# Strassen's seven block products in place of eight in a hybrid decoder step on one Trainium2 core

## The chip, the cores and the metric

The kernel runs on one core of a Trainium2 chip. A core has a matrix engine (TensorE, PE in the profile, with its weight loads as PEld), a vector engine (VectorE, DVE), a scalar engine (ScalarE, ACT), a general engine (GpSimd, POOL) and a queue that starts transfers (SyncE, SP). Each engine takes its own instructions in the order in which they were written, and waits on semaphores for the others. The metric is the device time of one execution in microseconds (us); less is better. Before the change it is 1356.34 us, the median of 3 runs from 1355.4 to 1358.23.

## The reference

One layer of a hybrid decoder, for 1024 prompt tokens and 32 sample tokens (8 sequences of 4), all in float32:

```python
def hybrid_layer(x, conv_state, ssm_state, mem_k, mem_v, ...):
    hn = rmsnorm(x, norm_g)
    proj = jnp.einsum('btd,de->bte', hn, w_in)      # 1024 -> 7696 columns
    gm_uv, gm_gate, ssm_z, ssm_xbc, ssm_dt, mem_q, mem_gate = jnp.split(proj, SPLIT_POINTS, axis=-1)
    a_out, v_rows = gmlp_branch(gm_uv, ...)          # gelu, layernorm of v, mix in 128-token chunks, u * mixed
    a_out = a_out * jax.nn.silu(gm_gate)
    b_out, ssm_new, conv_new = mamba2_branch(ssm_z, ssm_xbc, ssm_dt, conv_state, ssm_state, ...)
    c_out = memory_branch(mem_q, mem_gate, mem_k, mem_v)
    mixed = jnp.concatenate([a_out, b_out, c_out], axis=-1)
    y = x + jnp.einsum('bte,ed->btd', mixed, w_out)  # 3072 -> 1024 columns
```

`mamba2_branch` runs a causal convolution of width 4 over the 1536 columns of xbc, then an exact scan over 8 chunks of 128 tokens for 16 heads. `memory_branch` attends to 256 memory tokens, whose keys and values are projected here too. A final RMSNorm follows.

## The kernel before

**Products.** Every float32 operand of a large product is split by `split` (L104) into a float32r part H and a remainder L: ScalarE copies H, VectorE or GpSimd subtracts it. `gemm3` (L286) then does H*H, L*H and H*L for every 128 rows of the contraction, so three matmuls for each of its 8 steps of k. `gemmA` keeps the weights of one channel tile (128 channels) stationary and streams the 1056 tokens in three blocks of 352; `gemmB` keeps 128 tokens stationary and streams 256 channels. Weights arrive as 0.5 MB units (`w_load`), in the order of the list `wseq`, and are split one or two units ahead of their use (`w_tick`, `w_half`). The normed input xH, xL stays in SBUF.

**Stages.** In order: norm of the input with the z and dt columns (`z_unit`); the 12 channel tiles of xbc with the convolution (`conv_evac`, `conv_finish`); the 23 channel tiles of q, of the gate gg and of seven eighths of the gate mg, which `spill` sends to DRAM; v (`gemmB`, results stay in SBUF as vt); u with the mix of the gMLP (`mix`); the last tile of mg; the output projection of branch A (`outproj` with first=True), which puts y in DRAM; keys and values of the memory; the output projection of B, which adds to y; that of C with the residual and the final norm.

**Work beside the products.** `hook` is called after every step of k of a large product. It adds `pace["rate"]` to a counter, and for every whole one it steps a generator in `side`. Under q, gg and mg run, at 0.43 steps a hook, the chunked scan (`scan`: 16 chunk-and-group parts of 7 steps), the scan of the sample tokens (`sample_scan`) and the attention of the sample tokens against their caches (`sample_att`). The order of all instructions is that in which this Python code writes them (`manual_schedule`). So an instruction that waits on an engine holds all that stands behind it there.

**Banks.** `mm()` rotates over three PSUM banks for the large products; `sd()` over four for the side work.

**The lines that the steps touch.** In a channel tile of xbc, ScalarE takes each block out of PSUM twice (L646, L650), VectorE adds three shifted products of 1024 tokens (L659), and ScalarE applies Silu over the result (L664), which waits for them. In a part of the scan, GpSimd does the scale of the gated norm (L240, L241), the remainder of the scaled inputs (L110 xdL), the skip term (L775), the decay of the state (L877) and the scaled inputs of the next part (L782, whose buffer VectorE's L888 releases).

## Time and profile before

| what | value |
| --- | --- |
| time, median of 3 runs | 1356.34 us |
| span of the profiled execution | 1351.7 us |
| time around the span (median less span) | 4.6 us |
| TensorE busy | 1320.8 us, 98% |
| VectorE busy | 590.4 us, 44% |
| ScalarE busy | 496.5 us, 37% |
| GpSimd busy | 210.4 us, 16% |
| moved by DMA | 151.44 MB, 112 GB/s on average |

The profiled execution's own time is taken as its span of 1351.7 us and 4.6 us around it. Busy time of TensorE is counted from the start of a matmul to its modelled end; matmuls are pipelined, so the distance between the starts of two of them is shorter than the duration of one. The granted clock of TensorE reads 9 tenths or more in all 40 slices of the span.

### The profile page before, as it was taken

The numbers are of one execution on the slowest core, as the hardware profiler recorded it, in microseconds if no ns is written. First come the engines' busy times: TensorE is split into PE (matmuls) and PEld (weight loads), VectorE is DVE, ScalarE is ACT, GpSimd is POOL, SyncE is SP. The second block draws the span as 40 slices with busy tenths as digits, with TensorE's granted clock in tenths as the row PEclk, the third lists the DMA queues.
The fourth block names the chain that finished last, engine by engine and source line by source line (L and its number), as shares of the span: only waits on it lengthen the run. The fifth ranks groups of instructions, "written<-read, shape, count | busy, mean of one in ns | idle before, by whom it ended". The sixth has DMA issues, their size and how long they took to land. (4 is left out here: it accounts for less than half of the span.)

```text
span 1351.7 us, 22582 instructions
## 1 busy us (share of the span) xinstructions
PE 1320.8 (98%) x9231; PEld 1236.4 (91%) x9231; DVE 590.4 (44%) x943; ACT 496.5 (37%) x962; POOL 210.4 (16%) x274
## 2 busy tenths in 40 slices
PE   8999999999999999999999999999999889999996
PEld 7999999988888898888779999998999889999996
DVE  6212545566767632422112245345312646654543
ACT  6323444464545432222211124344313633322322
POOL 4200000043434424200000010002000600000122
PEclk9999999999999999999999999999999999999999
DMA  6223111122222245475551114221423565436432
GB/s 223 78 77 99 44 48 48 47 88 76 78 72 88 82 118 165 149 226 179 181 181 45 32 32 127 68 68 44 144 93 128 177 178 182 151 117 193 139 121 95
DMA packets 171595, 151.44 MB, mean 112 GB/s; under 512 B 13781, under 2 KB 155049, under 8 KB 171493
## 3 DMA queue, kind: packets, MB, share of 16 engines
q1 hardware_dynamic: 171492, 150.01, 36.1%
q8 instruction: 72, 1.18, 0.4%
q14 instruction: 31, 0.25, 0.1%
HBM read 111.97 MB, written 37.79 MB: 111 GB/s over the span
## 5 line engine op out<-in xcount | busy, mean ns | idle before, releaser
L290 PE MATMUL ps_mm<-xH,wh 128*128 128x352 f32 x1056 | 359.9, 341 | 0.0
L292 PE MATMUL ps_mm<-xH,wl 128*128 128x352 f32 x1056 | 339.6, 322 | 0.0
L291 PE MATMUL ps_mm<-xL,wh 128*128 128x352 f32 x1056 | 339.2, 321 | 0.0
L290 PEld LDWEIGHTS ps_mm<-xH,wh 128*128 128x128 f32 x1056 | 198.3, 188 | 25.3 <-issue 21.0
L291 PEld LDWEIGHTS ps_mm<-xL,wh 128*128 128x128 f32 x1056 | 199.0, 188 | 0.7
L292 PEld LDWEIGHTS ps_mm<-xH,wl 128*128 128x128 f32 x1056 | 198.4, 188 | 0.0
L110 DVE TENSOR_TENSOR wl<-wr,wh 128x1024 fp32r<-128x1024 f32 (+2 forms) x106 | 121.8, 1161 | 175.2 <-ACT wh L107 174.8
L290 PE MATMUL ps_mm<-wh,xH 128*128 128x256 f32 (+1 forms) x512 | 148.0, 289 | 0.0
L291 PE MATMUL ps_mm<-wl,xH 128*128 128x256 f32 (+1 forms) x512 | 146.4, 286 | 0.1
L292 PE MATMUL ps_mm<-wh,xL 128*128 128x256 f32 (+1 forms) x512 | 145.6, 284 | 0.3 <-DVE xL L110 0.3
L107 ACT ACTIVATE wh<-wr 128x1024 fp32r<-128x1024 f32 (+3 forms) x113 | 101.7, 915 | 36.2 <-PE ps_mm L291 14.2
L292 PEld LDWEIGHTS ps_mm<-wh,xL 128*128 128x128 f32 x512 | 98.1, 192 | 0.6 <-DVE xL L110 0.5
L290 PEld LDWEIGHTS ps_mm<-wh,xH 128*128 128x128 f32 x512 | 97.8, 191 | 0.4
L291 PEld LDWEIGHTS ps_mm<-wl,xH 128*128 128x128 f32 x512 | 97.7, 191 | 0.4 <-POOL wl L110 0.4
L701 ACT ACTIVATE gt<-ps_mm 128x352 f32<-128x352 f32 x72 | 33.0, 458 | 98.2 <-PE ps_mm L292 77.1
L290 PE MATMUL ps_mm<-aH,wh 128*128 128x384 f32 (+1 forms) x192 | 62.7, 327 | 1.9 <-ACT gt L1403 1.0
L290 PE MATMUL ps_mm<-bH,wh 128*128 128x384 f32 (+1 forms) x192 | 64.0, 334 | 0.0
L291 PE MATMUL ps_mm<-aL,wh 128*128 128x384 f32 (+1 forms) x192 | 63.0, 328 | 0.3
L292 PE MATMUL ps_mm<-bH,wl 128*128 128x384 f32 (+1 forms) x192 | 62.4, 325 | 0.2 <-DVE wl L110 0.2
L291 PE MATMUL ps_mm<-bL,wh 128*128 128x384 f32 (+1 forms) x192 | 62.5, 326 | 0.0
L292 PE MATMUL ps_mm<-aH,wl 128*128 128x384 f32 (+1 forms) x192 | 61.9, 323 | 0.0
L1720 POOL TENSOR_TENSOR xres<-xres,gfin 128x1536 f32<-128x1536 f32 (+3 forms) x6 | 14.4, 2392 | 231.6 <-ACT junk L1714 231.6
(385 smaller groups left out, 2472.8 us busy)
## 6 DMA issues: line engine op xcount, KB each, us to landing
wr<-in_w_in_dram SPq DMA_DIRECT2D x60, 512.0 KB
wr<-in_w_out_dram SPq DMA_DIRECT2D x24, 512.0 KB
kv<-in_cache_mem_k_dram SPq DMA_DIRECT2D x16, 512.0 KB
kv<-in_cache_mem_v_dram SPq DMA_DIRECT2D x16, 512.0 KB
y_d<-gt SPq DMA_DIRECT2D x32, 192.0 KB
q_d<-gt SPq DMA_DIRECT2D x24, 176.0 KB
gg_d<-gt SPq DMA_DIRECT2D x24, 176.0 KB
mg_d<-gt SPq DMA_DIRECT2D x24, 176.0 KB
```

The costliest lines, as they stand in the source:

```text
L107: ACT.activation(out=H, in_=raw, func=AF.Copy)
L110: leng.tensor_tensor(out=L, in0=raw, in1=rb(H), op=ALU.subtract)
L290: PE.matmul(out=ps, lhsT=lH, rhs=rH, start=(first and k == k0), stop=False)
L291: PE.matmul(out=ps, lhsT=lH, rhs=rL, start=False, stop=False)
L292: PE.matmul(out=ps, lhsT=lL, rhs=rH, start=False, stop=(last and k == k0 + kn - 1))
L701: ACT.activation(out=t[:, :BLK], in_=ps[:, :BLK], func=func)
L1720: eng.tensor_tensor(out=t[:, 0:nf, c0:c0 + w], in0=t[:, 0:nf, c0:c0 + w], in1=gc.unsqueeze(1).to_broadcast([128, nf, w]), op=ALU.mult)
```

## The change

Two channel tiles of weights (256 columns) now make a unit. Its 1024 x 256 weight block and the 1024 x 1024 input are cut into 2 x 2 blocks, and Winograd's form of Strassen's algorithm makes the four output blocks (128 channels x 512 tokens) from seven products of 512 rows of contraction instead of eight. There are 26 units: 6 for xbc, 4 each for q, gg, mg and u, and 4 for the output projection of branch A. `unit` does one. GpSimd makes the four sums of weight blocks (`u_prep`); ScalarE makes the H of all seven weight operands, and L comes from VectorE for operands 0, 3 and 6 and from GpSimd for 1, 2, 4 and 5 (`u_split`); VectorE joins the products with seven additions (`add`). The input's four sums T1 to T4 are made once, beside v (`x_sums`). The 32 sample tokens no longer ride in the products: each unit multiplies them in float32, in eight matmuls that use four column groups of the array (`samp_in`), and adds the four groups up a unit later (`samp_out`).

z and v come first now, and v's rows go to DRAM (`v_d`). The convolved xs, B and C go to DRAM (`xc_d`, `bc_d`) and come back part by part of the scan (`xk_load`); the gated rows of A, B and C go through `a_d`, `yb_d` and `c_d`. In the scan, the second half of the masks moves from VectorE to GpSimd (`sM`), the minimum and the transposed output of B from VectorE to ScalarE (`sE`, `y_T2`), and the rows of decays come by transfers that GpSimd starts (`r_rows`). The side work now runs at 0.8 to 1.0 steps a hook, over ten units.

```diff
+    XBC = [(0, 1), (2, 3), (8, 10), (4, 5), (6, 7), (9, 11)]
...
+    BANK = (0, 1, 2, 0, 2, 0, 1)
...
+    def u_prep(u, step):
+        if u >= len(useq):
+            return
+        if step == 0:
+            U.t[u] = [stp.tile([128, 4, 128], F32, tag=f"st{j}", name="wst", bufs=1) for j in range(2)]
+            t1, t2 = U.t[u]
+            POOL.tensor_tensor(out=t1, in0=A_(u, 2, 1), in1=A_(u, 2, 2), op=ALU.add)
+            POOL.tensor_tensor(out=t2, in0=t1, in1=A_(u, 1, 1), op=ALU.subtract)
+        else:
+            t1, t2 = U.t[u]
+            POOL.tensor_tensor(out=t1, in0=A_(u, 1, 1), in1=A_(u, 2, 1), op=ALU.subtract)
+            POOL.tensor_tensor(out=t2, in0=A_(u, 1, 2), in1=t2, op=ALU.subtract)
...
+    def u_split(u, j):
+        if u >= len(useq):
+            return
+        src = (lambda: A_(u, 1, 1), lambda: U.t[u][0], lambda: U.t[u][1], lambda: A_(u, 1, 2),
+               lambda: U.t[u][0], lambda: U.t[u][1], lambda: A_(u, 2, 2))[j]()
+        h, l = (stp.tile([128, 4, 128], F32R, tag=f"u{e}", name=f"u{e}", bufs=SR) for e in "hl")
+        split(src, h, l, ACT, POOL if j in (1, 2, 4, 5) else DVE)
+        U.hl[u, j] = (h, l)
...
+            for j in range(4):
+                PE.matmul(out=ps[32 * j:32 * j + 32, 0:256], lhsT=xs[:, 4 * r + j, :], rhs=R[r][:, j, :],
+                          start=(r == 0), stop=(r == 1), tile_position=(0, 32 * j))
+        se = gtp.tile([128, 256], F32, tag="se", name="se", bufs=1)
...
+        def add(out, ps, nm):
+            DVE.tensor_tensor(out=out, in0=ps, in1=keep[nm], op=ALU.add)
...
+        def add_fin(i, h, ps, nm):
+            t = dst(i, h)
+            add(t, ps, nm)
+            fin(i, h, t)
+        for j in range(7):
+            ps = banks[j] = mm_bank((BANK[j] + 2 * u) % 3)
+            wH, wL = U.hl.pop((u, j))
+            H, L = X[XN[j]]
+            gemm3(ps, lambda k: (wH[:, k, :], wL[:, k, :]), lambda k: (H[:, k, :], L[:, k, :]), 0, 4, True, True)
+            if j == 0:
+                ACT.activation(out=keep["m1"], in_=ps, func=AF.Copy)
+                u_prep(u, 1)
+                u_split(u, 3)
+            elif j == 1:
+                u_split(u, 4)
+                samp_out()
+                samp_in(u, xs, done)
+                u_free()
+            elif j == 2:
+                add(keep["u"], ps, "m1")
+                add(keep["x"], banks[1], "u")
+                u_split(u, 5)
+            elif j == 3:
+                add_fin(0, 0, ps, "m1")
+                u_split(u, 6)
+                u_prep(nx, 0)
+                u_free()
+            elif j == 4:
+                add(keep["u"], ps, "u")
+                add_fin(1, 1, banks[1], "u")
+                u_split(nx, 0)
+            elif j == 5:
+                add_fin(0, 1, ps, "x")
+                u_split(nx, 1)
+            else:
+                add_fin(1, 0, ps, "u")
+                u_split(nx, 2)
+            if mids is not None and j in mids:
+                mids[j]()
...
+            for nm, tg in (("B11", "m1"), ("B12", "u"), ("B22", "x"), ("B21", "st0")):
+                t = raw[nm] = (stp.tile([128, 512], F32, tag=tg, name=tg, bufs=1).rearrange("p (k t) -> p k t", k=4)
+                               if tg != "st0" else stp.tile([128, 4, 128], F32, tag="st0", name="wst", bufs=1))
+                H, L = XO[nm]
+                POOL.tensor_tensor(out=t, in0=rb(H[:, :, cs]), in1=rb(L[:, :, cs]), op=ALU.add)
+                yield
+            b11, b12, b21, b22 = (raw[nm] for nm in ("B11", "B12", "B21", "B22"))
+            for nm, out, a, b in (("T1", b11, b12, b11), ("T3", b12, b22, b12), ("T2", b22, b22, b11),
+                                  ("T4", b21, b21, b22)):
+                POOL.tensor_tensor(out=out, in0=a, in1=b, op=ALU.subtract)
+                yield
...
+    def conv_finish(ct):
+        raw = raws.pop(ct)
         o = VO["conv_b"] + ct
...
+        d = cvp.tile([128, NP], F32, tag="cd", name="cd", bufs=2)
+        ACT.activation(out=d, in_=raw[:, 3:3 + NP], func=AF.Identity, scale=cw(ct, 3), bias=vecs[:, o:o + 1])
...
+            DVE.scalar_tensor_tensor(out=d, in0=raw[:, j:j + NP], scalar=cw(ct, j), in1=d, op0=ALU.mult, op1=ALU.add)
+        ACT.activation(out=d, in_=d, func=AF.Silu)
+        SP.dma_start(out=xc_d[ct] if ct < 8 else bc_d[ct - 8], in_=d)
+        POOL.tensor_copy(out=csT[:, ct, 0:3], in_=raw[:, NP:NP + 3])
...
+    def conv_samples():
...
+        POOL.tensor_tensor(out=c4, in0=rs[:, :, :, 3:7], in1=w(3), op=ALU.mult)
+        POOL.tensor_tensor(out=c4, in0=c4, in1=vb(vecs[:, o:o + 12]), op=ALU.add)
         for j in range(3):
...
+            POOL.tensor_tensor(out=tm, in0=rs[:, :, :, j:j + 4], in1=w(j), op=ALU.mult)
+            POOL.tensor_tensor(out=c4, in0=c4, in1=tm, op=ALU.add)
...
     def sM(i, j):
         s_ = S[i]
-        DVE.tensor_tensor(out=s_.MT[:, 4 * j:4 * j + 4, :], in0=s_.MT[:, 4 * j:4 * j + 4, :],
+        (POOL if j else DVE).tensor_tensor(out=s_.MT[j], in0=s_.MT[j],
                           in1=s_.cbm.unsqueeze(1).to_broadcast([128, 4, 128]), op=ALU.mult)
...
+    def vh_norm(n):
+        h = QUAD[n % 4][1]
+        for j, op in enumerate((ALU.subtract, ALU.mult)):
+            POOL.tensor_tensor(out=vq[n], in0=vq[n], in1=VM[:, 4 * h:4 * h + 4, j:j + 1].to_broadcast([128, 4, 128]), op=op)
+    def ug_mul(n):
+        POOL.tensor_tensor(out=ugs[n], in0=ugs[n], in1=gq.pop(n), op=ALU.mult)
...
+    set_pace(0.8)
+    for i in range(4):
+        spill(2 * i, q_d, AF.Copy)
+    for i in range(4):
+        spill(2 * i, gg_d, AF.Copy)
+    for i in range(2):
+        spill(2 * i, mg_d, AF.Silu)
...
+    def a_split(nm):
...
+        OA[nm] = operand(xTp if nm[0] == "B" else xTp2, "x" + nm)
+        for k in range(2):
+            ks = slice(2 * k, 2 * k + 2)
+            split(AB.t[nm][:, ks, :], OA[nm][0][:, ks, :], OA[nm][1][:, ks, :], ACT, DVE)
+        if nm == "B21":
+            for k in range(4):
+                sub("T4", "B21", "T2", k)
```

On ScalarE, in the xbc stage, around the end of a channel tile. The rows are evictions (ps_mm to raw and xsT), Silu (L664) and the H of the weights (wh). Before:

```order
L646 ACTIVATE raw<-ps_mm 128x320
L648 ACTIVATE raw<-ps_mm 128x8x4
L650 ACTIVATE xsT<-ps_mm,vecs 128x352
L664 ACTIVATE xsT<-xsT 128x1056
L107 ACTIVATE wh<-wr 128x1024
L646 ACTIVATE raw<-ps_mm 128x352
```

The same place now, at the end of one unit and the start of the next (uh is the H of a weight operand, cd the convolved tile, m the first product's copy):

```order
L123 ACTIVATE uh<-wr 128x512 x2
L906 ACTIVATE cd<-raw,vecs 128x1024
L909 ACTIVATE cd<-cd 128x1024
L123 ACTIVATE uh<-wst 128x512
L906 ACTIVATE cd<-raw,vecs 128x1024
L909 ACTIVATE cd<-cd 128x1024
L123 ACTIVATE uh<-wst 128x512
L490 ACTIVATE m_3116<-ps_mm 128x512
L123 ACTIVATE uh<-wr 128x512
```

The H of the weights stood behind Silu before too, but for a product of a later channel tile; now two of them, for the second and third product of the next unit, each stand behind a Silu.

On GpSimd, in one part of the scan. Before:

```order
L240 TENSOR_SCALAR rstd<-ss 128x1
L241 TENSOR_TENSOR rstd<-rstd,mhalf 128x1
L110 TENSOR_TENSOR xdL<-xde,xdH 128x512
L775 TENSOR_TENSOR xsD<-xsD,dsk_b 128x512
L877 TENSOR_TENSOR hT<-hT,dec 128x512
L782 TENSOR_TENSOR xde<-xdt,te 128x512
```

Now (ul is the remainder of a weight operand, wst a sum of weight blocks, MT the masks):

```order
L271 TENSOR_SCALAR rstd<-ss 128x1
L272 TENSOR_TENSOR rstd<-rstd,mhalf 128x1
L126 TENSOR_TENSOR xdL<-xde,xdH 128x512
L1072 TENSOR_TENSOR xsD<-xsD,dsk_b 128x512
L126 TENSOR_TENSOR ul<-wst,uh 128x512
L858 DMA Rt<-acc_d 2x1024
L1114 TENSOR_TENSOR MT<-MT,cbm 128x512
L1173 TENSOR_TENSOR hT<-hT,dec 128x512
L1079 TENSOR_TENSOR xde<-xdt,te 128x512
L420 TENSOR_TENSOR wst<-wr 128x512
L421 TENSOR_TENSOR wst<-wr,wst 128x512
```

Between the scale (L272) and the scaled inputs of the next part (L1079) there now stand a mask, a transfer's issue and about every other time a remainder for the next product; sums of weight blocks follow.

## Rows read from the trace of the kernel before

**Rows 1.** Page, busy time of each engine: us, share of the span, instructions

```profile
PE 1320.8 (98%) x9231; PEld 1236.4 (91%) x9231; DVE 590.4 (44%) x943; ACT 496.5 (37%) x962; POOL 210.4 (16%) x274
```

**Rows 2.** Waits of TensorE: in total, times, longest, us

```profile
PE ps_sd L270 <- DVE xn L262: 4.6, 4, 1.8
...
PE ps_sd L1561 <- DVE qL L110: 3.5, 1, 3.5
```

**Rows 3.** Windows: busy us and instructions of each engine, granted clock, DMA share, GB/s

```profile
50.00:100.00 50.00, 50.00 (x422) 49.55 (x423) 5.20 (x10) 10.81 (x25) 4.67 (x6) 1.00 0.34 96
...
200.00:250.00 50.00, 50.00 (x317) 50.00 (x316) 24.93 (x33) 22.83 (x42) 2.07 (x16) 1.00 0.16 43
...
300.00:350.00 50.00, 50.00 (x378) 42.81 (x377) 33.44 (x58) 25.37 (x50) 18.64 (x22) 1.00 0.27 81
...
600.00:650.00 50.00, 50.00 (x351) 40.27 (x348) 10.33 (x14) 11.85 (x21) 0.00 (x0) 1.00 0.55 172
```

**Rows 4.** Timeline of TensorE, six 512-wide products in the scan: start, us, instruction

```profile
343.71 0.39 PE L797 MATMUL ps_sd<-hH,CH 128*128 128x512 f32 x1
...
344.86 0.40 PE L799 MATMUL ps_sd<-xdH,BL 128*128 128x512 f32 x1
```

**Rows 5.** Timeline of TensorE, float32 products in column groups

```profile
590.20 0.32 PE L292 MATMUL ps_mm<-xH,wl 128*128 128x352 f32 x1
...
590.45 1.06 PE L1137 MATMUL ps_acc<-kTb,qm 128*32 128x256 f32 x8
...
591.43 0.43 PE L290 MATMUL ps_mm<-xH,wh 128*128 128x352 f32 x1
```

**Rows 6.** Lines by form: count, busy us, mean ns, idle before and its releaser

```profile
L659 DVE SCALAR_TENSOR_TENSOR xsT<-raw,vecs,xsT 128x1024 f32<-128x1024 f32 x24 | 30.8, 1285 | 23.9 <-ACT xsT L650 21.4 <-POOL raw L629 2.0
...
L110 DVE TENSOR_TENSOR PL<-ps_sd,PH 128x512 fp32r<-128x512 f32 x16 | 11.0, 685 | 2.0 <-ACT PH L107 2.0
...
L664 ACT ACTIVATE xsT<-xsT 128x1056 f32<-128x1056 f32 x8 | 8.7, 1087 | 34.0 <-DVE xsT L662 34.0
...
L107 ACT ACTIVATE xdH<-xde 128x512 fp32r<-128x512 f32 x16 | 9.9, 616 | 0.0
...
L110 POOL TENSOR_TENSOR xdL<-xde,xdH 128x512 fp32r<-128x512 f32 x16 | 20.8, 1302 | 4.0 <-ACT xdH L107 4.0
...
L877 POOL TENSOR_TENSOR hT<-hT,dec 128x512 f32<-128x512 f32 x14 | 14.8, 1054 | 0.0
```

**Rows 7.** Timeline of DVE and POOL, one remainder of 128x128 beside POOL's xdL

```profile
352.45 1.21 DVE L110 TENSOR_TENSOR CL<-bcT,CH 128x128 fp32r<-128x128 f32 x1 [0.65 <-ACT CH L107]
...
352.22 1.29 POOL L110 TENSOR_TENSOR xdL<-xde,xdH 128x512 fp32r<-128x512 f32 x1
```

**Rows 8.** DVE and POOL, remainders of 128x384 side by side and alone

```profile
934.32 10.07 POOL L110 TENSOR_TENSOR aL<-vt,aH 128x384 fp32r<-128x384 f32 x8 [118.02 <-ACT aH L107]
...
L110 DVE TENSOR_TENSOR cL<-qT,cH 128x384 fp32r<-128x384 f32 x6 | 3.3, 551 | 0.0
...
L110 POOL TENSOR_TENSOR aL<-vt,aH x8: 1009/1330/1342, 934.3 to 943.1; 128x384 fp32r<-128x384 f32 x8
```

**Rows 9.** Timeline of POOL, one part of the scan

```profile
333.48 1.05 POOL L782 TENSOR_TENSOR xde<-xdt,te 128x512 f32<-128x512 f32 x1 [4.76 <-DVE xsD L888]
...
338.23 0.19 POOL L240 TENSOR_SCALAR rstd<-ss 128x1 f32<-128x1 f32 x1 [3.70 <-ACT sz L720]
...
338.50 0.55 POOL L241 TENSOR_TENSOR rstd<-rstd,mhalf 128x1 f32<-128x1 f32 x1
...
347.31 1.05 POOL L782 TENSOR_TENSOR xde<-xdt,te 128x512 f32<-128x512 f32 x1 [4.97 <-DVE xsD L888]
```

**Rows 10.** Sources: first and last start of the scan's and the state's transposes

```profile
L767 PE MATMUL ps_sd<-ident,xsT x64: 270/272/275, 267.2 to 458.2; 128*128 128x128 f32 x64
...
L1027 PE MATMUL ps_sd<-ident,hb x64: 270/272/301, 511.6 to 553.3; 128*128 128x128 f32 x64
```

**Rows 11.** Source of an issue on SP: min/median/max ns, first and last start us

```profile
L702 SPq DMA_DIRECT2D q_d<-gt x24: 319/320/575, 275.0 to 418.2; - x24
```

More of the change, by code (lines that the diff above doesn't have):

```diff
@@ new lines, in u_open, with samp_out @@
+    def u_open(u):
+        u_prep(u, 0)
+        for j in range(3):
+            u_split(u, j)
+    def samp_out():
+        if U.samp is None:
+            return
+        se, done = U.samp
+        U.samp = None
+        ps = sd()
+        for i in range(2):
+            PE.transpose(out=ps[:, i * 128:(i + 1) * 128], in_=se[:, i * 128:(i + 1) * 128], identity=ident)
+        r = gtp.tile([128, 2, NS], F32, tag="sr", name="sr", bufs=2)
+        DVE.tensor_reduce(out=r, in_=ps[:, 0:256].rearrange("p (i g t) -> p i t g", i=2, g=4), axis=AX.X, op=ALU.add)
+        done(r)
@@ L533, in hybrid_step, with x_sums @@
     s_ctx.close()
+    xt2_ctx = ExitStack()
+    xTp2 = xt2_ctx.enter_context(tc.tile_pool(name="xTp2", bufs=1, side="right"))
+    for nm in ("T1", "T2", "T3", "T4"):
+        XO[nm] = operand(xTp2, "x" + nm)
+    def x_sums():
+        for q in range(4):
+            cs = slice(128 * q, 128 * q + 128)
+            raw = {}
+            for nm, tg in (("B11", "m1"), ("B12", "u"), ("B22", "x"), ("B21", "st0")):
[8 more added lines that the diff above has]
+                POOL.tensor_tensor(out=out, in0=a, in1=b, op=ALU.subtract)
+                yield
+                H, L = XO[nm]
+                split(out, H[:, :, cs], L[:, :, cs], ACT, DVE)
+                yield
@@ L677, in hybrid_step, with next_unit @@
+    nu = [0]
+    def next_unit(dst, fin, done, mids=None, X=XO, xs=xsr):
+        unit(nu[0], X, xs, dst, fin, done, mids)
+        nu[0] += 1
+    side.add(dt_chain(cvp))
+    side.add(conv_state())
+    pace["acc"] = 0.0
+    set_pace(0.3)
+    for cts in XBC:
+        next_unit(conv_dst(cts), conv_fin(cts), conv_done(cts))
     side.drain()
@@ L830, in scan @@
         sz_load(0)
-        yield
-        yield
-        yield
+        xk_load(0)
+        lt_make(0)
+        lt_make(1)
+        for _ in range(5):
+            yield
         sA(0)
@@ L1022, in s1 @@
             hbt = hb_t.pop(b)
-            hTb = sp2.tile([128, 1024], F32, tag="hTb", name="hTb", bufs=2)
+            hTb = [sp2.tile([128, 512], F32, tag="hTb", name="hTb", bufs=3) for _ in range(2)]
             for j in range(2):
@@ L1075, in sample_scan @@
             yield
-        for _ in range(5):
+        for _ in range(4):
             yield
@@ new lines, in hybrid_step, with a_open @@
+    for m in range(4):
+        u_unit(m)
+    AB = WS()
+    OA = {}
+    def a_open():
+        side.drain()
+        g_ctx.close()
+        G.c0.close()
+        AB.ctx = ExitStack()
+        p = AB.ctx.enter_context(tc.tile_pool(name="abuild", bufs=1))
+        AB.t = {nm: p.tile([128, 4, 512], F32, name="a" + nm) for nm in ("B11", "B12", "B22", "B21", "T1", "T2")}
+        AB.t["T3"] = AB.t["B12"]
+        AB.t["T4"] = AB.t["B21"]
+        side.add(a_build())
+        pace["acc"] = 0.0
+        set_pace(1.0)
@@ L1497, in k_T @@
         yield
+    for n in range(3):
+        loadB(n)
     n = 0
```

901 lines of the change are left out of this document (531 added, 370 removed).

## Prediction

> **What bounds the kernel now.** I read the busy times first: TensorE is at work for 98% of the span [rows 1]. The table of its waits shows that there is nearly nothing else: the longest entries are 4.6 and 3.5 us in total [rows 2]. The chain that ended last covers only the last few us, so it says nothing here; the windows say more. In each of the four that I took TensorE is busy for all of its 50 us at the full granted clock, while VectorE, ScalarE and GpSimd have time left: in the scan 33.4, 25.4 and 18.6 of 50 us [rows 3]. So the span is TensorE's own work, laid end to end. Taking work from TensorE shortens it, as long as no other engine becomes late. That is the question here, because the change takes from the engine that has no time and gives to the three others, GpSimd above all.
>
> **What TensorE saves.** A pair of channel tiles took 2 x 3 x 8 x 3 = 144 matmuls of 352 columns. In the window from 200 to 250, which holds almost only those, 317 instructions take 50 us: 0.158 us each, so 22.7 us a pair [rows 3]. A unit has 7 x 4 x 3 = 84 matmuls of 512 columns. Six such in the scan start 1.15 us apart over five steps, 0.23 us each [rows 4]; a line through 0.158 us for 352 and 50/422 = 0.118 us for 256 columns [rows 3] gives 0.223. I take 0.225, so 18.9 us. The saving is 3.8 us in each of 26 units: 99 us (the output projection's blocks of 384 and 288 columns are as many columns in as many matmuls).
>
> **What TensorE pays back.** The sample tokens cost eight float32 products of 256 columns a unit, in four column groups. The trace has four such in two column groups: from 590.36 (a pitch after 590.20) to 591.43, 1.07 us [rows 5]. Eight at that price are 2.1 us; if four groups overlap twice as well as two, 1.1. I take the middle, 1.6, and 0.2 for two transposes (272 ns each in rows 10, of which most overlaps their neighbours). That is 1.8 us x 26 = 47 us (34 to 60). The Trainium skill, "TensorE: Matmul & The Clock Gate", Part 3 (packing small matmuls), gives 2.38 times for three column tiles, by which the cost would lie near the lower end; no row here shows more than two groups.
>
> TensorE alone would then need 1351.7 - 99 + 47 = 1300 us. A product is now 12 x 0.225 = 2.7 us, and a unit of TensorE's own 20.7 us.
>
> **xbc: two waits in every unit.** The new order on ScalarE puts Identity and Silu of a finished channel tile ahead of the H of the next unit's second operand, and those of the other tile ahead of the third's. Silu waits for VectorE's three shifted products, as it does now: ScalarE sat idle 34.0 us before 8 of them [rows 6]. Before, that hit weights needed a channel tile later; now it hits the next product but one. From the end of a unit's sixth product: addition 0.69, Identity 1.09 (priced as Silu), three products of 1.285, Silu 1.09, H 0.62: 7.35 us, and GpSimd's L, 1.30, at 8.65 [rows 6]. TensorE has done the seventh product and the next unit's first at 5.4. The second needs L from its third matmul on and ends at 8.65 + 10 x 0.225 = 10.9 instead of 8.1: 2.8 late. The second tile's Identity, products, Silu and H stand behind that: 7.35 + 6.66 = 14.0, L at 15.3, the third product ends at 17.55. Without this wait it would be 10.9 + 1.8 + 2.7 = 15.4: 2.15 late. Together 4.95 us, after each of 6 units (the sixth in q's first): 30 us. Then eight GpSimd operations of 128x384 for the samples' convolution, 1.01 us each [rows 8], come ahead of the first q unit's sums of weights: 15.3 + 8.1 + 2.6 (two sums) + 1.3 = 27.3 for a remainder wanted at 20.7, 6.6 late. Sum 36 us. If only the first wait of each unit is left it is 17; if GpSimd and VectorE also block each other (below) up to 50.
>
> **The scan: GpSimd.** Its 16 parts start 191.0 / 15 = 12.7 us apart [rows 10], with 7 steps at 0.43 a hook, so 16.3 hooks of 3 x 0.158 = 7.7 us; a part's own TensorE work is 5.0 us. At 0.8 a unit of 28 hooks steps 22.4 times, 3.2 parts: TensorE needs 20.7 + 16.0 = 36.7 us a unit, 11.5 a part. The scan's 122 steps last 5.45 units. GpSimd now makes four sums and four remainders a unit, 8 x 1.30 = 10.4 us, and for a part 0.74 for the scale [rows 9], 1.30 for xdL, three broadcast products of 1.05 [rows 6], a mask between 1.05 and 1.30 (say 1.2) and a transfer's issue. That one no row has on GpSimd; I take 0.32, the issue on SP [rows 11], with 1.30 as the upper bound. That is 6.7 a part, 21.5 a unit, 31.9 together.
>
> To this come waits for the port that VectorE and GpSimd seem to share: a 128x128 remainder on VectorE took 1.21 us and ended with GpSimd's xdL [rows 7]. Eight remainders of 128x384 on GpSimd took 10.07 us with VectorE's at their side, 1.26 each where one alone takes 1.01, for 0.55 us of VectorE [rows 8]: 0.45 us for each us of VectorE. VectorE's operations with both inputs in SBUF are 11.8 us a unit (three remainders of 0.685, and four of 0.69 and one of 0.29 in each of 3.2 parts), so 5.3 us: GpSimd 37.2 against TensorE's 36.7. It also cannot use all of its time: its queue stops at the scale and at xde, 3.70 and 4.76 us in one part [rows 9]. From the scale to xde are 9.1 of 13.8 us now, 66%; of 11.5 us that is 7.6. In it GpSimd must do 5.0 us of the scan's work, two operations of the unit and 1.5 us of waits: 9.1. So 1.5 us late in each part, 24 us for 16. If the other engines' queues hide it all, 0; with no overlap at all and the dear issue, 57.
>
> **The rest.** u: GpSimd 10.4 + 8.4 (eight products with the mean and scale) + 5.2 + 2.2 for the port = 26.2 us, TensorE 20.7 + 16 float32 products at 0.22 = 24.2; 2 us x 4 = 8 (0 to 18). The last two mg units: 20.8 + 16 subtractions 20.8 + 6.3 for the port = 47.9 against 41.4, and 4 MB read back: 8 (0 to 14). Sample scan: 8 MB go in and out in 41.7 us [rows 10]; its 23 steps took 53 hooks or 25 us of products and so 16.5 of its own work; 15 steps at 0.85 leave 17.6 hooks of 0.675, 12 us, so 28 in all, or 285 GB/s with the weights on top, and 172 GB/s was already a DMA share of 0.55 [rows 3], 313 at full; 10 (0 to 15). Start of the memory's products: two 0.5 MB units split only then, 4 (0 to 5). The added DRAM trips of v, xs and the gated rows I cost at nothing else: they are issued by SP, and windows with a DMA share of 0.16 and 0.27 [rows 3] hide them. The x sums beside v, 32 x 1.30 = 42 us on GpSimd, fit v's 32 x 24 matmuls at 0.118 = 91 us.
>
> **Sum.** 1300 + 36 + 24 + 8 + 8 + 10 + 4 = 1390 us of span, and 4.6 us around it (1356.34 less 1351.7): 1394 us, 2.8% slower than the median of 1356.34. Own range 1360 to 1430.
>
> **Rivals.**
> 1. TensorE stays the bound outside xbc. A remainder made after one product is needed two products later, and in the scan a product with its side work lasts 5 us; if this depth swallows GpSimd's delay, only xbc's 36 us are left: 1300 + 36 + 4.6 = 1341, and 1308 with the lower ends of xbc and the samples. For it: GpSimd stood waiting for others twice in a part, 8.5 of 13.8 us [rows 9], and TensorE's waits have no entry of GpSimd among the longest [rows 2]. Against: GpSimd would have to work all of its time. It decides where the waits outside xbc fall below 1351.7 - 1336 = 16 us. Faster; chance 0.25.
> 2. VectorE and GpSimd take strict turns. The row with 1.21 us looks like it [rows 7], the eight in 10.07 us less so: full turns would make 8 x 1.56 = 12.5 [rows 8]. Then the scan costs 31.9 + 11.8 - 36.7 = 7.0 us a unit, 38 in all, u 18 and mg 14 instead of 24, 8 and 8: 1394 + 30 = 1424 us. Chance 0.15. The Trainium skill, "SBUF — State Buffer", section "SBUF: two separate sides", states this as the rule: the shared pair is an exclusive lock for an operation with two SBUF inputs against one of GpSimd that reads SBUF.
> 3. No change, gain and waits equal: 1356; 0.04. That the change doesn't do what it says I leave out: the order shows the 512-wide products.
>
> **How the numbers follow.** The forecast has 0.56, the rivals 0.25, 0.15 and 0.04. What a measurement of this kernel can tell from no change is about 0.2%, 2.7 us. Faster 0.25, same 0.04, slower 0.71. The range 1315 to 1455 leaves out the best cases of rival 1 and those in which the port and the issue are both dear.
>
> **What would show it.** In xbc a unit lasts 25 to 26 us, TensorE idle before its second and third product, released by ScalarE and GpSimd, and ScalarE idle ahead of Silu. In the scan GpSimd is busy above 85% and parts start 12.5 to 13.5 us apart. The samples' eight products span 1.1 to 2.1 us. I am wrong if TensorE is still busy above 95%; or if it idles elsewhere, above all for transfers.

## The result: 1512.6 us, 11.6% slower

The changed kernel takes 1512.56 us (median of 4 runs, 1505.02 to 1520.15) where the kernel before took 1355.87 beside it: 1.116 times as long, 95% interval 1.1113 to 1.1208. Slower was right; 1394 was 119 us short, and the range ended at 1455.

The page after, in the order of [rows 1]: busy us of each engine, share of the span, instructions.

```profile
span 1503.1 us, 21893 instructions
...
PE 1320.4 (88%) x8139; PEld 1090.1 (73%) x8139; DVE 749.7 (50%) x1110; ACT 551.0 (37%) x1090; POOL 653.8 (43%) x604
...
PEclk9999998899888899989989999999799999999998
```

TensorE is busy for as long as before, with 1092 instructions fewer. So it works slower (10 of the 40 slices have a granted clock below 9 tenths, where before none had) and stands idle for 183 us instead of 31. The waits of TensorE after, in total, times, longest, answer to [rows 2], whose longest entries were 4.6 and 3.5 us:

```profile
PE ps_sd L1063 <- DMA bc<-bc_d: 16.9, 1, 16.9
PE ps_mm L325 <- POOL ul L126: 15.7, 12, 4.2
PE ps_mm L323 <- ACT uh L123: 14.9, 7, 2.3
PE ps_sd L1104 <- ACT sz L1012: 14.4, 9, 2.2
PE ps_sd L1631 <- POOL vh L1616: 12.8, 7, 3.8
PE ps_sd L1094 <- DVE xdt L1069: 11.2, 10, 3.1
```

No single wait holds the loss: ScalarE, VectorE, GpSimd and a transfer each have some. Windows by stage (busy us of PE, PEld, DVE, ACT and POOL, granted clock, DMA share, GB/s) stand against the 50.00 busy us at a clock of 1.00 of [rows 3]; they are xbc with the step to the scan, the scan, u, the last mg units, the last stage:

```profile
228.00:417.00 189.00, 147.13 (x651) 110.11 (x649) 110.31 (x139) 64.31 (x93) 91.15 (x104) 0.88 0.24 75
417.00:700.00 283.00, 225.91 (x1411) 160.13 (x1411) 164.42 (x247) 136.56 (x308) 171.86 (x174) 0.90 0.33 98
905.00:1010.00 105.00, 94.41 (x493) 75.14 (x491) 61.61 (x79) 45.32 (x75) 89.97 (x74) 0.98 0.47 143
1010.00:1080.00 70.00, 55.49 (x259) 42.41 (x259) 40.62 (x40) 26.57 (x41) 56.59 (x40) 0.88 0.40 135
1372.00:1503.00 131.00, 106.32 (x652) 103.48 (x650) 49.74 (x97) 34.37 (x83) 21.07 (x14) 0.93 0.45 146
```

The whole span can be split in three: TensorE idle, time lost to the lower clock (the busy time of each window of 1 us, times what its granted clock lacks of 1), and the rest, which is TensorE's work at the full clock.

| | work at full clock | idle | lost to the clock | span |
|---|---|---|---|---|
| before | 1314.0 | 30.9 | 6.8 | 1351.7 |
| after | 1256.5 | 182.7 | 63.9 | 1503.1 |
| difference | -57.5 | +151.8 | +57.1 | +151.4 |

How a wait and the lower clock belong together is seen in one unit of xbc (timeline of TensorE: start, us; in brackets the idle time before and its releaser). The products of 512 columns stand 0.23 us apart, as the 0.23 of [rows 4]; then come two waits, and behind them 0.43:

```profile
313.64 0.39 PE L324 MATMUL ps_mm<-xB11L,uh 128*128 128x512 f32 x1
313.87 0.39 PE L325 MATMUL ps_mm<-xB11H,ul 128*128 128x512 f32 x1
316.50 0.50 PE L323 MATMUL ps_mm<-xT1H,uh 128*128 128x512 f32 x1 [2.25 <-ACT uh L123]
316.84 0.42 PE L324 MATMUL ps_mm<-xT1L,uh 128*128 128x512 f32 x1
317.86 0.79 PE L325 MATMUL ps_mm<-xT1H,ul 128*128 128x512 f32 x1 [0.60 <-POOL ul L126]
318.45 0.63 PE L323 MATMUL ps_mm<-xT1H,uh 128*128 128x512 f32 x1
318.88 0.63 PE L324 MATMUL ps_mm<-xT1L,uh 128*128 128x512 f32 x1
```

The windows around it (columns as above) show the clock at 1.00 up to the waits, at 0.50, which is 1.2 GHz, behind them, and back at 2.4 GHz some 6 us later:

```profile
314.00:317.00 3.00, 0.75 (x4) 0.30 (x2) 1.44 (x2) 2.12 (x3) 0.47 (x1) 1.00 0.08 34
317.00:320.00 3.00, 2.40 (x7) 1.76 (x6) 2.29 (x2) 0.58 (x1) 2.00 (x2) 0.51 0.35 143
320.00:323.00 3.00, 3.00 (x12) 1.98 (x15) 1.57 (x2) 1.36 (x2) 0.00 (x0) 0.50 0.00 0
323.00:326.00 3.00, 3.00 (x23) 1.84 (x20) 1.72 (x3) 1.22 (x3) 2.71 (x2) 0.85 0.46 180
```

One of the four executions of b1 and one of b4 was a disturbed one: their times below are medians of the other three, and b1's profile is not used.

### The profile page after: what moved, and what is told of

Read it like the earlier page. It is cut to its first block, busy times and chain, and to the rows that moved or that the text cites. A ratio compares the mean times of both kernels' runs of the same rounds, so it can differ in the third digit from the quotient of the medians.

```text
span 1503.1 us, 21893 instructions
## 1 busy us (share of the span) xinstructions
PE 1320.4 (88%) x8139; PEld 1090.1 (73%) x8139; DVE 749.7 (50%) x1110; ACT 551.0 (37%) x1090; POOL 653.8 (43%) x604
## 5 line engine op out<-in xcount | busy, mean ns | idle before, releaser
L126 POOL TENSOR_TENSOR ul<-wst,uh 128x512 fp32r<-128x512 f32 x104 | 137.5, 1324 | 233.0 <-ACT uh L123 188.0
L126 DVE TENSOR_TENSOR ul<-wr,uh 128x512 fp32r<-128x512 f32 x78 | 82.4, 1056 | 89.0 <-ACT uh L123 89.0
L123 ACT ACTIVATE uh<-wst 128x512 fp32r<-128x512 f32 x104 | 64.9, 624 | 97.9 <-POOL wst L420 47.3
L126 DVE TENSOR_TENSOR wl<-wr,wh 128x512 fp32r<-128x512 f32 (+3 forms) x53 | 59.3, 1146 | 64.2 <-ACT wh L123 63.7
L123 ACT ACTIVATE uh<-wr 128x512 fp32r<-128x512 f32 x78 | 48.5, 622 | 38.3 <-PE ps_mm L324 32.8
L323 PE MATMUL ps_mm<-xT1H,uh 128*128 128x512 f32 x104 | 47.7, 458 | 13.3 <-ACT uh L123 13.3
L908 DVE SCALAR_TENSOR_TENSOR cd<-raw,vecs,cd 128x1024 f32<-128x1024 f32 x36 | 46.3, 1285 | 22.5 <-issue 11.2
L123 ACT ACTIVATE wh<-wr 128x512 fp32r<-128x512 f32 (+3 forms) x60 | 47.0, 813 | 24.6 <-DVE go L477 8.6
L323 PE MATMUL ps_mm<-xT2H,uh 128*128 128x512 f32 x104 | 48.3, 465 | 1.8 <-ACT uh L123 1.6
L325 PE MATMUL ps_mm<-xT1H,ul 128*128 128x512 f32 x104 | 46.4, 446 | 3.7 <-POOL ul L126 3.7
L325 PE MATMUL ps_mm<-xB22H,ul 128*128 128x512 f32 x104 | 43.4, 418 | 4.2 <-POOL ul L126 4.2
```

The source lines that it names most:

```text
L123: ACT.activation(out=H, in_=raw, func=AF.Copy)
L126: leng.tensor_tensor(out=L, in0=raw, in1=rb(H), op=ALU.subtract)
L323: PE.matmul(out=ps, lhsT=lH, rhs=rH, start=(first and k == k0), stop=False)
L325: PE.matmul(out=ps, lhsT=lL, rhs=rH, start=False, stop=(last and k == k0 + kn - 1))
L908: DVE.scalar_tensor_tensor(out=d, in0=raw[:, j:j + NP], scalar=cw(ct, j), in1=d, op0=ALU.mult, op1=ALU.add)
```

## The experiments

Sixteen kernels, each the changed kernel with the edit shown. Time is the median in us, the ratio is to the kernel before on the same chip. Gains in the text are differences of medians, from 1512.6 where nothing else is said. The changed kernel's own runs span 15 us and its ratio runs from 1.111 to 1.121, so by time alone a1, b2, b3, d1 and d2 cannot be told from it, nor c3 from c2; of these the profiles decide.

| run | time | ratio, 95% interval |
|---|---|---|
| a6 a wait of known length in v | 1572.5 | 1.161 (1.156 to 1.166) |
| a1 xbc's finish put off | 1502.6 | 1.110 (1.108 to 1.113) |
| b4 xbc's finish in pieces | 1489.8 | 1.101 (1.096 to 1.106) |
| d1 products filled into xbc's wait | 1509.9 | 1.117 (1.113 to 1.120) |
| a2 scan started later | 1524.2 | 1.126 (1.123 to 1.129) |
| b3 samples' convolution in pieces | 1508.1 | 1.115 (1.112 to 1.117) |
| a4 GpSimd's remainders left out | 1464.8 | 1.084 (1.080 to 1.088) |
| b1 scan's order | 1494.3 | 1.103 (1.100 to 1.107) |
| b2 scan at pace 0.6 | 1506.2 | 1.114 (1.111 to 1.118) |
| d2 products filled into the scan's waits | 1512.7 | 1.117 (1.115 to 1.120) |
| e1 last stage's splits later | 1496.7 | 1.108 (1.106 to 1.110) |
| c1 Strassen undone in 16 units, T1 in the place of B12 | 1461.3 | 1.079 (1.076 to 1.082) |
| c2 three orders (b1, b3, b4) | 1470.2 | 1.086 (1.081 to 1.090) |
| c3 c2 and GpSimd's load moved | 1466.1 | 1.082 (1.079 to 1.085) |
| e3 c3 and e1 | 1444.6 | 1.069 (1.065 to 1.072) |
| e2 Strassen undone in 22 units, T1 in the place of B12, b1, b3, b4, e1 | 1414.4 | 1.047 (1.042 to 1.052) |

### What a wait costs where TensorE sets the time (a6)

```diff
...
+            if t in (1, 4, 7):
+                ACT.activation(out=gap[:, 0:256], in_=ps, func=AF.Copy)
+                for _ in range(4):
+                    ACT.activation(out=gap, in_=gap, func=AF.Copy)
+                psg = sd()
+                PE.transpose(out=psg[:, 0:128], in_=gap[:, 0:128], identity=ident)
```

> The changed kernel with a wait of known length put into the v stage, which runs at the full clock: behind 12 of its 36 row blocks a chain of five copies on ScalarE, which TensorE has to wait for with a transpose, about 3 us each. It prices a wait by itself, beside 256-wide products and without any 512-wide ones. Theory W: each wait is followed by some us at 1.2 GHz; 12 x (3.1 + about 2) = 61 us, 1573 us, with granted clocks of 0.50 after each wait in v. Rival I (the low clock belongs to the 512-wide products): 12 x 3.1 = 37 us, 1549 us, and v stays at 1.00.

60 us for 12 waits. The wait's row, and windows around one of them (its transpose starts at 170.66):

```profile
PE ps_sd L728 <- ACT gap L726: 41.8, 12, 5.8
```

```profile
166.00:170.00 4.00, 1.48 (x13) 1.27 (x11) 0.00 (x0) 2.30 (x5) 0.00 (x0) 1.00 0.62 195
170.00:172.00 2.00, 1.34 (x11) 1.35 (x12) 1.00 (x2) 1.39 (x3) 0.00 (x0) 0.95 0.13 48
172.00:175.00 3.00, 3.00 (x16) 3.00 (x16) 0.12 (x1) 0.00 (x0) 1.28 (x1) 0.50 0.04 12
175.00:178.00 3.00, 3.00 (x27) 3.00 (x27) 1.12 (x2) 0.90 (x2) 0.91 (x1) 0.97 0.13 44
```

Each wait was 3.5 us of idle time (3.2 to 5.8) and cost 5.0: here the low clock follows waits of this length, without any product of 512 columns. The Trainium skill, "TensorE: Matmul & The Clock Gate", Part 1, prices a throttled stretch at its time multiplied by what the clock lacks; the 1.5 us beside 3 us at 0.50 agree.

### xbc: the queue moves, the pace stays (a1, b4, d1)

a1 issues a channel tile's whole finish during the next unit; b4 cuts it into five operations, one or two behind each product; d1 changes no order and fills the wait.

```diff
# a1
-                conv_finish(cts[i])
+                late_c.append(cts[i])
...
+        next_unit(..., {0: conv_late, 2: conv_late})
# b4
+                pieces.extend(conv_finish(cts[i]))
+        next_unit(..., {0: fine(2), 1: fine(2), 2: fine(2), 3: fine(1), 5: fine(1), 6: fine(2)})
# d1, ahead of the second product of units 1 to 6
+                fill(9)
```

> The changed kernel with one edit: in the xbc stage the Identity, three shifted products and Silu of a finished channel tile are issued during the next unit (after its first and its third product) and no longer ahead of the H of its second and third operand. Same work. Theory W (each wait is paid twice: as idle time, and as TensorE at the 1.2 GHz level for some us after it): the xbc units fall from 26.5 to about 21 us, five of them, the granted clock there goes back to 1.00, time 1512 - 30 = about 1482 us. Rival I (a wait costs only its idle time; the low clock comes from the 512-wide products themselves): five times 2.9 us, 1498 us, and the clock in xbc stays below 0.95. Rival G (GpSimd and the shared port set the unit's pace): within 5 us of 1512.

> The changed kernel with xbc's finish of a channel tile cut into its five operations, one or two behind each product of the next unit, so that neither ScalarE nor VectorE stands in it for more than 2.6 us. Same work. Theory V (after the putting off of the whole finish TensorE waited for VectorE's sums, which stood behind three products of 1.3 us and hold the PSUM banks): five units at 21.5 us, 1512 - 25 = about 1487 us, the clock in xbc above 0.98. Rival G (VectorE and GpSimd are simply too busy in xbc, in whatever order): units of 24 us as when the whole finish was put off, about 1500 us.

> The changed kernel with 9 products of 512 columns added ahead of the second product of the units 1 to 6 (2.0 us each, into a bank that nothing reads), where TensorE waits 2.25 us for ScalarE: 12 us of work added and nothing taken away. Theory W (the low clock follows from TensorE's own idle time): the clock in xbc rises from 0.90 to 0.98 or more, the units fall from 26.5 to about 25 us, time 1512 - 8 = about 1504 us. Rival L (the clock is lowered by the load of all engines together): more work lowers it further, 1512 to 1524 us, clock in xbc 0.90 or less.

a1 gave 10 us by the medians, and 8 in its five units of xbc (135.3 us where the changed kernel takes 143.6), not 30. In xbc ScalarE's 14.9 us of TensorE's waits became VectorE's: the sums that free a PSUM bank now stood behind the shifted products.

```profile
PE ps_mm L323 <- DVE raw L477: 16.5, 5, 3.6
PE ps_mm L325 <- DVE ul L126: 6.1, 1, 6.1
PE ps_mm L323 <- ACT uh L123: 2.0, 1, 2.0
```

b4 gave 23: units of 23.0 to 23.7 us in the steady part where the changed kernel has 25.9 to 26.6 (the first products of the samples are one unit apart), and the clock there at 1.00. That is between its two theories, and still 3 us above TensorE's own 20.3 (84 products at 0.227 and the samples' part). d1 decides what the low clock was worth. Its windows of one unit, 366 to 378, and the same stretch of the unit without filling (367 to 379), each kernel in its own fence:

```profile
366.00:372.00 6.00, 5.71 (x24) 4.07 (x23) 4.06 (x4) 2.44 (x3) 0.78 (x1) 1.00 0.09 38
372.00:378.00 6.00, 3.83 (x29) 2.54 (x29) 3.85 (x3) 1.95 (x4) 1.71 (x3) 1.00 0.13 51
```

```profile
367.00:373.00 6.00, 3.12 (x11) 1.89 (x10) 3.73 (x4) 2.71 (x3) 2.47 (x2) 0.89 0.21 87
373.00:379.00 6.00, 5.33 (x31) 3.31 (x30) 3.28 (x5) 2.58 (x4) 2.47 (x2) 0.82 0.22 89
```

The clock came back, so load did not lower it. But the time did not fall as theory W had it: TensorE, faster now, waited 1.62 us for ScalarE and 0.62 for GpSimd at the next product, where the changed kernel waits 0.63 at most:

```profile
377.95 0.50 PE L323 MATMUL ps_mm<-xT2H,uh 128*128 128x512 f32 x1 [1.62 <-ACT uh L123]
379.31 0.74 PE L325 MATMUL ps_mm<-xT2H,ul 128*128 128x512 f32 x1 [0.62 <-POOL ul L126]
```

The last three units still took 25.9 to 28.1 us. Together they hold 7.6 us more of TensorE's work than the changed kernel's, 5.0 less lost to the clock and 0.9 less idle, and are 1.7 longer. ScalarE and VectorE set the pace of xbc; there the low clock only used up time that TensorE would have waited.

### Where the scan starts (a2, b3)

The 16.9 us for bc begin earlier than the transfer: SP issued the scan's first loads at 412.54 to 413.38, because their tiles take the memory of the samples' convolution, which ended on GpSimd at 412.5.

```diff
# a2
     def scan():
+        for _ in range(14):
+            yield
# b3: rs in another pool, and the eight operations as pieces
+        spill(2 * i, q_d, AF.Copy, {j: cs_p.pop(0) for j in range(7) if cs_p} if 0 < i < 3 else None)
```

> The changed kernel with one edit: the side chain of the scan starts 14 hooks later and then waits 6 instead of 5, so its first loads are issued after the samples' convolution on GpSimd has ended, whose memory they take over. Same work. Theory W: the 16.9 us for which TensorE waits for bc at the first transposes go, with some 6 us at the low clock behind them: 1512 - 20 = about 1492 us. Rival D (the chain is only moved, and the 14 hooks are paid at its end, where it is drained without cover): within 5 us of 1512.

> The changed kernel with one edit: the samples' convolution (8 GpSimd operations, a copy and a Silu) is issued in pieces behind the products of q's second and third unit, its tiles in memory that the scan does not take over. Same work. Theory M (the scan's first loads wait for the memory of that convolution, and its Silu blocks ScalarE for 9 us): TensorE's wait for bc shrinks from 16.9 to below 8 us, with the clock behind it and no step moved: 1512 - 15 = about 1497 us. Rival S (the loads still wait for the last channel tile's Silu and store): within 5 us.

a2 was 12 us slower. The wait for bc is gone, but from 395 to 440 TensorE waits 10.6 us for ScalarE's H, behind the Silu that still waits for that convolution, and the 14 steps come back at the end: in the window 880 to 935, where the chain is drained, the clock is 0.81. b3 cut the wait for bc to 9.6 us, and the stretch from the last sample products of xbc to the first of q from 43.4 to 36.1; of that the median shows 4 us, which is within the spread. What is left is the last tile's trip through DRAM (stored there and read back): its Silu ends at 405.15, SyncE issues the load at 408.82, and TensorE goes on at 412.45.

### The scan: not GpSimd's load (a4, b1, b2, d2)

```diff
# a4: one old remainder U.l0 in place of those of operands 2, 3, 5, 6
-        split(src, h, l, ACT, POOL if j in (1, 2, 4, 5) else DVE)
+            ACT.activation(out=h, in_=src, func=AF.Copy)
+            l = U.l0
# b1: hT *= dec on GpSimd ahead of sM(i + 1, 1), and y_T2 ahead of gate_norm
# b2
-    set_pace(0.8)
+    set_pace(0.6)
# d2, in sE ahead of the second exponent, and ahead of the product with the state
+            fill(6)
+                fill(4)
```

> Left out: the four remainders of a unit that GpSimd makes (second, third, fifth and sixth operand; one old remainder is used in their place), 5.2 us of GpSimd a unit. TensorE's work is the same. Theory of the prediction (GpSimd is full in the scan, u and the last mg units): some 40 us and the clock behind them go, 1512 - 60 = about 1450 us. Rival Q (TensorE waits in the scan for queues that stand in a bad order, not for a full GpSimd; only the waits that name GpSimd's remainders go, 6.6 + 5.9 + 3.2 us, with the clock behind them): about 1490 us.

> The changed kernel with two edits of order in the scan and the same work: GpSimd's scaling of the state hT is issued ahead of its mask product (which waits for ScalarE's exponential), and ScalarE's scaled copy of the finished part (which frees a PSUM bank) ahead of the Square that waits for VectorE. Theory Q (the scan's waits are those of queues in a bad order): VectorE's 30.5 us of waiting for hT and TensorE's 19.8 us for the bank go, with the low clock behind them; parts 15.5 -> 13.5 us apart, 1512 - 30 = about 1480 us. Rival P (the chain of one part, from its transposes to its state, is as long as before, and a part's steps now stand closer in TensorE's order than that chain lasts): the waits move to the next link, within 8 us of 1512.

> The changed kernel with the pace of the side chain in the scan at 0.6 steps a hook instead of 0.8: one and a third times as many products between a part's steps. Rival P: parts still start about 15.5 us apart, TensorE fills its idle time with the units' products (some 7 units beside the scan instead of 5.4), idle there falls from 57 to below 25 us and the clock there rises to 0.97; but the later side work is then drained at the end with less cover, so the time falls by 20 to 40 only, about 1480 us. Theory Q: every part has the same waits, 57 us of idle time stay, parts 17.5 us apart, and the time rises to about 1530 us.

> The changed kernel with products added in every part of the scan, into a bank that nothing reads: 6 of 512 columns ahead of the second exponent's product, where TensorE waits 1.2 to 2.2 us in most parts, and 4 ahead of the product with the state, where it waits about 1 us: 34 us of work added. Theory P + W (parts 15.5 us apart whatever TensorE does, and the low clock follows from its idle time): the clock in the scan rises from 0.91 to 0.96 or more, parts stay 15 to 16 us apart, time between 1495 and 1512 us. Rival L: the clock stays or falls, and the 34 us come on top where the wait was shorter than the filling: 1530 to 1546 us.

With a fifth less work on GpSimd (512 us instead of 654) the time fell by 48 us, but only some 8 of them in the scan, whose parts went from 15.5 to 15.0 us; xbc's units are 7 us shorter, u's 14 and the last two of mg 6. In u GpSimd was the limit: from the first to the last product with v it took 89 us instead of 103, and TensorE is busy for nearly all of a4's window there:

```profile
905.00:1010.00 105.00, 104.10 (x571) 83.51 (x571) 60.54 (x86) 45.67 (x76) 80.16 (x65) 1.00 0.53 168
```

In the scan (417 to 650, the changed kernel) GpSimd waited itself, 43.6 us of it for ScalarE's exponential:

```profile
POOL MT L1114 <- ACT MT L1110: 43.6, 13, 8.7
POOL rstd L271 <- ACT sz L997: 16.3, 9, 3.6
```

and VectorE for what stood behind that on GpSimd:

```profile
DVE hT L1184 <- POOL hT L1173: 28.3, 8, 6.6
DVE ul L126 <- ACT uh L123: 19.3, 11, 2.9
```

b1 took that coupling apart by order alone: 18 us, between the 30 of a theory of queues and the under 8 of a fixed chain. c2, which has b1's order, waits less for hT, and its parts are 14.5 us apart:

```profile
DVE hT L1211 <- POOL hT L1198: 5.4, 2, 4.4
```

d2 added some 31 us of TensorE's work (1287 at the full clock, as in the table, instead of 1256) and no time that can be measured; parts went to 15.75 us and the clock from 0.90 to 0.94 (417 to 650). From the start of its first part to that of its last TensorE has 29.6 us more work, 17.8 less idle time, 8.2 less lost to the clock, and 3.6 us more in all. b2 answered neither theory: parts 17.0 us apart, and what the fuller scan saved was lost at the drain, where the side work that is left runs on without enough products beside it (830 to 890: idle for 16 us instead of 3).

### The last stage (e1)

```diff
-            if b < 2 and ct < 7:
-                c_split(b + 1, ct, 1 if ct < 6 else 2)
+            if b < 2 and ct >= 2:
+                c_split(b + 1, ct - 2, 1)
+            if b < 2 and ct == 7:
+                c_split(b + 1, 6, 2)
```

> The changed kernel with one edit in the last stage: the split of the next token block, which waits for its transfer from DRAM, is issued two products later (and so behind the splits of two more weight blocks on ScalarE). Same work. Theory T (ScalarE's queue: the split of cr waits for its transfer, 61.8 us in 11 waits, and the split of the weights that the next product needs stands behind it): TensorE's waits of 5.7 and 2.9 us for woH and woL go, with some us at the low clock, 1512 - 10 = about 1502 us. Rival B (the transfers of that stage, 23.7 MB, are simply too many at once, and the weights themselves come late): within 4 us.

The last stage took 130.8 us where it had taken 115.4, with products of the same shape. It now reads its right-hand operand back from DRAM; ScalarE waits for that ahead of the weights' split. Its waits in the stage, in the changed kernel and then in e1:

```profile
ACT cH L123 <- DMA cr<-c_d: 61.8, 11, 18.2
```

```profile
ACT cH L123 <- DMA cr<-c_d: 19.8, 5, 14.8
```

TensorE's wait of 5.7 us for woH is not in e1's list. e1 gave 16 us and a stage of 116 us. A trip that the prediction cost at nothing was worth all of its 15 us, through one in-order queue.

### Do the mends add up, and what is Strassen worth (c2, c3, e3, c1, e2)

```diff
# c1, units below 16: 8 phases (i, kh, h) of 4 k-steps, no sums
+            gemm3(ps, ..., 0, 4, kh == 0, kh == 1)
# c3, vh_norm on VectorE; remainders of units 20 to 22 on VectorE
+            DVE.tensor_scalar(out=vq[n][:, c, :], ..., op0=ALU.subtract, op1=ALU.mult)
```

> The changed kernel with the three edits of order together: the scan's order on GpSimd and ScalarE, the samples' convolution in pieces, xbc's finish in pieces. Each alone gave 18, 4 and 19 us. Theory W: they act at different places and add up, 1512 - 41 = about 1471 us; TensorE's idle time falls from 183 to about 145 us and its granted clock rises to 0.955. Rival C (what one edit saves, the next queue in the chain takes): 1485 us, no better than the best alone by over 10 us.

> The kernel of the three orders, and in u the gated rows' norm on VectorE (one operation a tile and 128 columns) instead of two on GpSimd, and the four remainders of the last two mg units and the first of the output projection on VectorE. Same work. Theory of the prediction for these two stages (GpSimd is full there): the waits for vh (12.8 us) and for the remainders from 1035 to 1085 (9.2 us) go, with the clock behind them: 30 us under the kernel of the three orders, about 1441 us. Rival V (VectorE becomes the full one there): under 10 us.

> The changed kernel with all mends and Strassen in every unit: the three orders, the balance in u and the last mg units, the later splits in the last stage. If the mends add up: 1466 - 8 = about 1458 us. Rival C: 1466 us.

> Strassen undone in 16 of the 26 units (xbc, q, the gates and the first two of mg), all else as changed: two channel tiles by two token halves by two halves of K, 8 products of 4 k-steps with 512 columns in place of 7, four weight blocks split instead of seven, no sums of weights, four evictions instead of six additions and two copies; the same DRAM trips, samples' products and side chain (0.7 steps a hook, which is as many steps a unit). B12, whose memory is given up after v, is stood in for by T1. TensorE's work is 16 x 2.7 = 43 us more. Theory W (Strassen's bookkeeping makes the waits, and each is paid twice): xbc units 24 us and, beside the scan, idle time of 25 instead of 57 us; the time falls by 30, to about 1480 us. Rival R (the waits come from the rest of the change: the DRAM trips, the scan's new order, the sample products, the denser steps): they stay, and the 43 us come on top: about 1550 us.

> Strassen undone in all 22 units on x (B12 stood in for by T1, as in the run with 16), kept in the first output projection, with the orders of the scan, of xbc's finish and of the samples' convolution mended and the last stage's splits later; the DRAM trips and the samples' products stay. TensorE's work is 22 x 2.6 = 57 us more than in the changed kernel. Theory W: 1461 (Strassen undone in 16) - 20 (orders) - 8 (last stage) - 5 (u) = about 1428 us, idle time about 95 us, and what is left over before is the samples' products (26 us) and the trips. Rival C (the orders and the undoing hit the same waits): 1450 us or more.

The orders add up (42 us, 41 expected), though the wait at the scan's start, which b3 had cut, is back: 15.7 us for bc in c2 (b4 by itself has 19.7). c2 finishes the last unit's two tiles behind all products of xbc, and bc is loaded after that. Moving GpSimd's load to VectorE gave 4, within the spread, not 30: the waits for vh (13.2 us in c2) went and waits for VectorE's sums came. c3, from 866 to 1100:

```profile
PE ps_mm L323 <- DVE u L477: 12.6, 2, 7.5
...
PE ps_sd L1659 <- DVE vh L1643: 2.2, 3, 0.7
```

e3 is the best version with Strassen everywhere. It took the last stage's mend better than expected (21 us, not 8), and it is still 93 us behind the kernel before.

c1 is the sharpest. It leaves the values of B12 out (T1 is read in its place, in products of the same shape), and its 0.7 steps a hook are as many steps a unit as in the changed kernel. It is 51 us faster with 39 us more of TensorE's work (1295.6 at the full clock). Windows of its xbc and scan, to be held against 0.88 and 0.90 above:

```profile
280.00:380.00 100.00, 91.80 (x452) 73.23 (x450) 47.83 (x54) 31.84 (x42) 18.31 (x31) 0.97 0.26 87
390.00:600.00 210.00, 183.27 (x1233) 134.80 (x1231) 106.91 (x188) 113.85 (x258) 111.48 (x120) 0.99 0.37 110
```

Its xbc units take 23.2 us, its parts 13.8. So Strassen's sums, remainders and additions cost these 16 units some 90 us of waits and low clock for 39 us of products. e2 has about as much of TensorE's work as the kernel before (1309 and 1314) and takes 62 us longer: that is left, without any Strassen on x, of the trips, the orders, the side work, the samples' products and the output projection's four units. No run divides it among them.

## Why the prediction was wrong

- **TensorE's work: right.** -52 us forecast (99 less 47), -57.5 measured. The pitch was 0.227 us, not 0.225. The eight sample products took 1.07 us, the lower end of 1.1 to 2.1; I took 1.6. The row answers to [rows 5] (a float32 product leaves two records here: 16 for eight products, as 8 for four there):

```profile
375.40 1.07 PE L463 MATMUL ps_sd<-wr,xsr 128*32 128x256 f32 x16
```

- **xbc, unit of 25 to 26 us: right in the steady part** (25.9 to 26.6), and right in how. The first wait, 2.8 in the forecast, is 2.25 for ScalarE's H and 0.60 for GpSimd's L, both in the second product. The second, 2.15 at the third product, shows at the full clock: 1.62 and 0.62 in d1. In the changed kernel the low clock fills most of that time. Missed: the first two units beside the dt chain, 31.6 and 33.2 us, some 13 us; with the finish in pieces (b4) they take 27.0 and 25.0.
- **"Late for a remainder wanted at 20.7, 6.6": the place was right, the sufferer was not.** The samples' convolution held the scan's memory and ScalarE, and TensorE stood 16.9 us: 10 us more.
- **The scan, "1.5 us late in each part, 24 us for 16": the step that failed most.** GpSimd was busy for 172 of 283 us, 61%, not above 85%, and parts stood 15.5 us apart, not 12.5 to 13.5: some 40 us more. I added up GpSimd's own work between its two stops (9.1 us against 7.6) and made TensorE wait for the difference. What delayed TensorE was a ring of in-order queues, in which each engine waits for the next: GpSimd 43.6 us for ScalarE's exponential, VectorE 28.3 for what stood behind that on GpSimd. A fifth less work on GpSimd took 0.5 us off a part (a4), order alone 1.0 (c2), and more work on TensorE added 0.25 (d2). A part takes 4.0 us more than the 11.5 that I forecast for TensorE alone; which links hold the other 3, no run took apart. The transfer's issue on GpSimd took 0.62 us (median of 16), not 0.32.
- **u, the last mg units, the sample scan, 8 + 8 + 10:** idle 10.6 (905 to 1010), 14.5 (1010 to 1080) and 6.8 us (700 to 869). In u the limit was GpSimd, as forecast (busy for 90 of 105 us, and a4). Its price was too low: four units took 29.3 us each (the sample products at 902.28 and 1019.46), not 26.2. The start of the memory's products, 4, was right: waits of 1.8 and 2.3 us for wh and wl.
- **"The added DRAM trips I cost at nothing else": wrong** by 15 us in the last stage alone (e1).
- **The clock was in no term.** I said that TensorE ran at its full clock everywhere and kept that for the kernel after. 64 us are lost to it, 57 more than before. The 38 of them in xbc and the scan (228 to 700) cost next to nothing of their own (d1, d2), since other engines set the pace; where TensorE sets it, each wait cost 1.4 times its idle time (a6).
- **Rivals.** Rival 1 (TensorE stays the bound outside xbc) is out: busy 88%. Rival 2 (strict turns) was right that the two engines shut each other out, and wrong to book all of it on GpSimd (below). A plan in which other engines pace several stages was not among my cases, so the range could not hold the time.

The parts of the miss that have a number: scan 40, xbc's first units 13, the scan's start 10, u 12, last stage 15, the last two mg units 8 (57.0 us where 49.4 was forecast), the first output projection 12 (31.2, 22.4 and 20.5 us between its units' sample products; 20.7 forecast). a4 took 6 us off the mg units; beyond that no run took the last two apart.

## What to carry to other kernels

When a change takes work from the engine that has no time left and hands it to three in-order queues, price the longest ring of waits through them, stage by stage; a sum of each engine's work is only a lower bound. Where TensorE still sets the pace, count a new wait of the lengths met here (2.9 to 5.8 us) with the low clock behind it. And an operation that waits for a transfer must not stand in a queue ahead of one that the next product needs.
